# Two transformer blocks on one core: the experts' scatter and the next gather are emitted behind the following pair's gates

## The chip, the core and the metric

The kernel runs on one core of a Trainium2 chip. The metric is the device time of one execution in microseconds; the median of the runs is compared. The engines are TensorE (PE; its weight loads are listed apart as PEld), VectorE (DVE), ScalarE (ACT), GpSimd (POOL) and SyncE (SP), which issues most of the DMA transfers between the device's memory (HBM) and the on-chip SBUF. Matrix products land in PSUM.

## The reference, cut to what matters

The program is one block with two linear mixers and a mixture of experts, then a second block of two layers with attention and feed-forward. The change touches the experts alone: 256 tokens of 1024 features, 32 experts, of which each token takes the four with the largest logits. In words of the reference, per expert `e` on its rows `xb`:

```python
gu  = xb @ w_gu[e] + b_gu[e]
glu = jnp.minimum(gu[:, :D_EXPERT], SWIGLU_LIMIT)
lin = jnp.clip(gu[:, D_EXPERT:], -SWIGLU_LIMIT, SWIGLU_LIMIT)
act = glu * jax.nn.sigmoid(SWIGLU_ALPHA * glu) * (lin + 1.0)
return (act @ w_down[e] + b_down[e]) * p[:, None].astype(h.dtype)
```

The rows are added up at their tokens, and the sum times a gate `g2` is added to the residual. All weights are float32: 8 MB of gate and up weights and 4 MB of down weights an expert.

## The kernel before, in words

`phase1` is the mixer of the first block, `moe` the experts, `phase2` the second block. The change lies in `moe` (lines 1131 to 1389).

The 32 experts go in 16 pairs, 0 to 15, and two pairs make a block of four experts. Each expert has 64 slots for its tokens (`CAP`); the two experts of a pair lie side by side in the 128 rows of a matmul's output. What happens to a block and its pairs:

- **Gather** (lines 1323 to 1339). Two selection matrices `S` (VectorE, line 1325) of 128 tokens by 256 slots; then eight products of the normalized tokens (in two parts, `hl` and `hh`) with `S` on TensorE (line 1336), each into one of the two PSUM tiles `tr`, from which `scaled` (ScalarE line 1242, VectorE line 1244, in turn) writes an eighth of `xg`. `xg` is a tile of its own for odd blocks and lies in `resB` for even ones.
- **Gate and up** (line 1353). Eight steps, each of two pieces of weights (one of either expert, [128, 2048]) against an eighth of `xg`, into the PSUM tiles `gt` and `lt`; then the bias as a product (line 1357). These are the pair's gates.
- **Activation** (`swiglu`, lines 1250 to 1256). VectorE clamps `gt` to `g` and `lt` to `act`, ScalarE does three functions on `sg`, VectorE two more products. Eight transposes on TensorE (line 1263) and two copies on ScalarE (line 1264) turn the result to `aT`.
- **Down** (line 1373). Four steps of two pieces each, into `yd`.
- **Scatter** (lines 1266 to 1283). Two transposes of the slots' weights `sp` (line 1271), a copy to `spT`; VectorE multiplies `yd` by `g2` into `ys` (line 1277); four products of `spT` with `ys` (line 1280), each into one of the two tiles `tr`, and after each an addition to the residual `resA` on VectorE (line 1281).

The program emits this pair after pair: gather (in every second pair), gates, activation, down, scatter. A scheduler places the instructions of an engine in an order of its own, by its forecast of when each is ready, and an engine runs its own in that order. Where a conditional stands the order can't be mixed across it: ahead of pair 8 a branch (`overflow`, line 1292) looks whether an expert has more than 64 tokens; for these inputs it is not entered. The output biases of the experts are added in pair 6 (`biases`), and small preparations for the second block stand behind pairs 9, 11 and 13.

The weights come in 384 pieces of 1024 KB, which SyncE issues in order (line 1102) into a ring of 14 buffers (11 of `mring`, three of an older pool); a load waits until the products that read its buffer's last piece are done. Three more pieces are loaded ahead into a pool of their own at the start.

Of the kernel before, what the change touches and what calls it, by code (L numbers as in the profile page):

```python
# [9 lines left out]
F32 = mybir.dt.float32  # L10
# [10 lines left out]
# ---------------------------------------------------------------- constants that depend on shapes alone  # L21
def shape_constants():
# [9 lines left out]
    C["cum"] = np.concatenate([blk * (i[None] >= p[:, None]), blk * (i[None] <= p[:, None])], 1)   # within a chunk  # L32
    C["blk64"] = blk
    C["tri"] = (p[:, None] < i[None, :]).astype(np.float32)      # earlier tokens
    C["iota"] = np.broadcast_to(i.astype(np.float32), (128, 128)).copy()
    # rotary: swap of the halves of 64 dims, cos and signed sin over the 272 positions
# [7 lines left out]
def position_constants():  # L44
    """cos / signed sin [128, 2, 272], retention decays [128, 4, 656], and the buckets of the distances."""
# [4 lines left out]
    cos, sin = np.cos(ang).T, np.sin(ang).T                       # [32, T]  # L50
# [4 lines left out]
    dec = np.where(i >= j, np.exp(lg[:, None, None] * np.maximum(i - j, 0)), 0.0)     # [4, j, i]  # L55
# [4 lines left out]
    # table over m: distance m - 127, m = 0 .. 399  # L60
# [22 lines left out]
class K:  # L83
    """Handles shared by the parts of the program."""
# [5 lines left out]
    def c(self, pool, *names):  # L90
        """Load constants that lie side by side."""
        o = CONST_OFF[names[0]][0]
        n = CONST_OFF[names[-1]][0] + CONST_OFF[names[-1]][1] - o
        t = pool.tile([128, n], F32, name=self.nm("cst"), tag=self.nm("cst"), bufs=1)
        self.nc.sync.dma_start(t, self.a["cst"][:, o:o + n])
        r = [t[:, CONST_OFF[x][0] - o:CONST_OFF[x][0] - o + CONST_OFF[x][1]] for x in names]
        return r if len(r) > 1 else r[0]
# [6 lines left out]
class Halves:  # L104
    """[128, 8, 256] float32r as two tiles of four."""
# [9 lines left out]
def row_bcast(ap, parts, n):  # L115
    """A DRAM vector read onto every one of `parts` partitions."""
    return bass.AP(tensor=ap.tensor, offset=ap.offset, ap=[[0, parts], [1, n]])


def rsqrt_small(k, pool, out, v, n, parts=128, tag="rs", full=None):  # L120
    """out = v ** -0.5 on a small tile, with one Newton step after exp(-0.5 ln v)."""
# [15 lines left out]
LOW = -44.0                                                    # below it a sigmoid is under 1e-19, and Ln's range ends  # L137


def sigmoid(k, out, x):  # L140
    """out = 1 / (1 + exp(-x)) for x >= LOW."""
# [6 lines left out]
def split_hl(k, hi, lo, x):  # L148
    """x (float32) = hi + lo exactly, hi and lo in float32r."""
# [4 lines left out]
def mm3(nc, out, terms, start, stop):  # L154
    """The sum of float32 products w x as float32r ones, first those of the w's high parts.

    terms: (w high, w low, x high, x low, whether w is the stationary operand)."""
# [9 lines left out]
def load_w(k, src):  # L167
    """Weights of up to 1024 elements a partition: rows in tiles of 128."""
# [6 lines left out]
def parts(k, w):  # L175
    """The two float32r parts of a weight tile of 1024 elements a partition."""
# [7 lines left out]
# the order of the delta rule's steps. E: a group's decays on their way, P: the product of the next convolution, K, Q, V:  # L184
# convolutions, M: system matrices, X: a part of their inverses, H: what a head's scan takes, S: a step of the scan of two
# heads; k, q, v: projections of the linear attention, m: half of the modulation
DELTA_ORDER = "EkPPKPKPKPKMmXXXXXXXXXPQPQPVVHHkqSSSSSSSSPPQPQPVVHHSSSSSSSSEkPPKPKPKPKMXXXXXXXXXPQPQPVmVHHSSSSSSSSkPPQPQPVqqVHHSSSSSSSSqvv"
# the order of the linear attention's steps: D a head's decays and states, O its output, v values of a further head,
# S, G, R, b gates, B the normalized output
# [3 lines left out]
def phase1(k, A, B):  # L193
    """The mixer of the first block: x + g1*y by token in 2048 of 2176 columns of A; B is free after it.

    With it the norm's factor of a token (k.rstd), scale and shift of a feature (k.scale, k.shift) of the experts' input
    and the router's logits. Returns the experts' weights, with the first on their way."""
# [27 lines left out]
    # ------------------------------------------------ loads  # L225
# [3 lines left out]
    def big(shape, dt=F32):  # L229
        """2048 elements a partition."""  # L230
# [37 lines left out]
    adt = one.tile([128, 2, 16], F32, name="adt")                # a_log and dt_bias on every partition  # L268
# [9 lines left out]
    # ------------------------------------------------ modulation  # L278
# [14 lines left out]
    # ------------------------------------------------ normalized tokens, feature-major: [ctx | lat]  # L293
# [43 lines left out]
    def proj_fm(src, xh, xl):  # L337
        """128 output columns feature-major, [128, tokens of xh]."""
# [5 lines left out]
    def proj_tm(src, tiles, xh, xl, evac):  # L344
        """256 output columns token-major for the token tiles; evac(token tile, psum)."""
# [14 lines left out]
    # ------------------------------------------------ beta, decay gates, low-rank gates  # L360
# [12 lines left out]
    ba = B[0:48, 0:512]                     # beta's argument, and from row 32 the decay's  # L373
# [7 lines left out]
    tok = one.tile([128, 4, 3, 16], F32, name="tok")             # G, beta, exp(last - G) by token  # L381
# [6 lines left out]
    nc.scalar.activation(e1, e1, AF.Ln)                          # -ln beta  # L388
    # g = -exp(a_log) * softplus(a + dt_bias), log1p with its rounding made good
# [4 lines left out]
    nc.scalar.activation(e2, e2, AF.Exp, scale=-1.0)             # e = exp(-|x|)  # L394
    nc.vector.tensor_scalar_add(u1, e2, 1.0)                     # u = 1 + e
    nc.scalar.activation(g1, u1, AF.Ln)
    nc.vector.scalar_tensor_tensor(e2, u1, -1.0, e2, op0=ALU.add, op1=ALU.subtract)      # (u - 1) - e
# [5 lines left out]
    nc.vector.tensor_scalar_max(g1, g1, -104.0)                  # exp is zero there, and sums stay exact enough  # L403
# [8 lines left out]
    gb = one.tile([128, 4, 24], F32, name="gb")                  # G and G + ln beta (backward), to be turned to rows  # L412
# [50 lines left out]
    # ------------------------------------------------ convolution and its gate  # L463
# [11 lines left out]
    def conv_cols(ct):  # L475
        """Columns ct of q, k, v (24 tiles); its product may have been taken up before."""
# [42 lines left out]
    oa = B[:, 0:2048].rearrange("p (h t w) -> p t h w", h=8, t=2)            # its place is taken over by the experts' input  # L519
# [1506 lines left out]
```

## Time and profile before

| | |
|---|---|
| median of 3 runs | 2528.71 us (2528.28 to 2530.66) |
| the profiled execution, first to last instruction | 2534.7 us |
| mean granted TensorE clock | 0.958 of full speed |
| TensorE busy | 2342.3 us, 92% |
| VectorE, ScalarE, GpSimd busy | 1242.1, 924.1 and 118.7 us |
| moved by DMA | 605.9 MB, 239 GB/s in the mean |

The page gives for the profiled execution the busy time of each engine and, for 40 equal slices of 63.4 us, tenths of busy time. The profile shows a float32 matmul as two rows of TensorE, so the 72 gate and up matmuls of a pair (with the bias) are 144 rows. Experts run from about 750 to 1745 us: slices 12 to 28. The profile has no time of its own besides the span; the runs' median lies 6.0 us below it.

### The profile page before, as it was taken

What the parts mean: (1) busy time and instruction counts of PE and PEld (TensorE: products, weight loads), DVE (VectorE), ACT (ScalarE), POOL (GpSimd) and SP (SyncE); (2) the same over time, 40 slices, a digit from 0 to 9 for tenths busy, and PEclk for the clock granted to TensorE, in tenths of its full rate; (3) what the DMA queues carried; (4) which work ended last, traced back from release to release, by engine and by line L of the source; (5) the groups of instructions that cost most, each with busy time, mean ns of one, the idle gap of its engine ahead of it and who ended that gap; (6) DMA issues with size and microseconds to landing.
All of it is one profiled execution on the core that took longest, in us unless ns stands there. A gap on an engine that the chain in (4) does not pass through costs nothing.

```text
span 2534.7 us, 36527 instructions
## 1 busy us (share of the span) xinstructions
PE 2342.3 (92%) x14474; PEld 1550.9 (61%) x14475; DVE 1242.1 (49%) x2717; ACT 924.1 (36%) x1956; POOL 118.7 (5%) x156
## 2 busy tenths in 40 slices
PE   6699879999989999999899999998999999999998
PEld 3476557789873333333333333335878999878998
DVE  4988896677561111121211111114766556766655
ACT  4556555567430101010101010103455545455544
POOL 0112122000010000000000000000010000010000
PEclk8889988999989999999999999999999999999999
DMA  7522330234979999999899999995434555524563
GB/s 281 136 78 57 119 112 29 59 92 117 285 288 386 396 416 410 416 406 397 346 416 412 416 398 416 392 416 168 124 85 140 182 167 155 158 87 134 185 183 100
DMA packets 290349, 605.90 MB, mean 239 GB/s; under 512 B 26038, under 2 KB 218681, under 8 KB 254332
## 3 DMA queue, kind: packets, MB, share of 16 engines
q1 hardware_dynamic: 283236, 595.24, 64.1%
q10 hardware_dynamic: 6280, 7.80, 1.2%
q8 instruction: 116, 1.90, 0.3%
q0 software_dynamic: 656, 0.46, 0.1%
q14 instruction: 61, 0.50, 0.1%
HBM read 602.30 MB, written 1.15 MB: 238 GB/s over the span
## 4 chain that ended last, share of the span: by engine, by line
PE 33%; issue 14%; DVE 2%; ACT 1%; POOL 0%; DMA 0%; POOLq 0%; ACTq 0%; DVEq 0%
PE qm L164 13%; PE yd L1373 5%; PE gt L1353 4%; PE lt L1353 4%; PE tr L1280 1%; PE tr L1336 1%; PE gt L1357 0%; PE tr L1263 0%; PE qm L1759 0%; PE qm L1758 0%; DVE g L1250 0%; DVE act L1256 0%; PE ql L1822 0%; POOL bs L1775 0%; ACT sg L1254 0%
## 5 line engine op out<-in xcount | busy, mean ns | idle before, releaser
L150 ACT CAST wh<-w 128x1024 fp32r<-128x1024 f32 (+2 forms) x318 | 318.6, 1002 | 298.0 <-PE qm L164 203.2
L151 DVE TENSOR_TENSOR wl<-w,wh 128x1024 fp32r<-128x1024 f32 (+2 forms) x318 | 369.9, 1164 | 38.5 <-ACT wh L150 36.8
L164 PE MATMUL qm<-uh,wh 128*128 128x272 f32 (+2 forms) x1008 | 260.2, 292 | 0.1
L1373 PE MATMUL yd<-w,aT 128*64 128x512 f32 x1024 | 259.0, 637 | 0.9 <-ACT aT L1264 0.6
L164 PE MATMUL qm<-ul,wh 128*128 128x272 f32 (+2 forms) x1008 | 258.1, 289 | 0.0
L1250 DVE TENSOR_SCALAR g<-gt 128x1024 f32<-128x1024 f32 x16 | 19.6, 1224 | 409.5 <-PE gt L1357 353.9
L1252 ACT ACTIVATE sg<-g 128x1024 f32<-128x1024 f32 x16 | 16.9, 1057 | 538.5 <-DVE g L1250 538.5
L164 PEld LDWEIGHTS qm<-uh,wh 128*128 128x128 f32 (+1 forms) x1008 | 188.6, 187 | 7.6 <-issue 5.1
L164 PEld LDWEIGHTS qm<-ul,wh 128*128 128x128 f32 (+1 forms) x1008 | 189.2, 188 | 2.5 <-issue 0.7
L1353 PE MATMUL gt<-w,resB 128*64 128x512 f32 x512 | 183.3, 596 | 0.0
L1353 PE MATMUL lt<-w,resB 128*64 128x512 f32 x512 | 181.3, 593 | 0.6 <-DVE act L1251 0.6
L1353 PE MATMUL gt<-w,xg 128*64 128x512 f32 x512 | 178.3, 595 | 0.0
L1373 PEld LDWEIGHTS yd<-w,aT 128*64 128x64 f32 x1024 | 78.8, 148 | 161.4 <-issue 152.6
L1353 PE MATMUL lt<-w,xg 128*64 128x512 f32 x512 | 177.5, 593 | 0.0
L164 PE MATMUL qm<-uh,wl 128*128 128x272 f32 (+2 forms) x1008 | 147.7, 287 | 0.0
L164 PE MATMUL mm<-hTh,wh 128*128 128x256 f32 (+1 forms) x384 | 131.6, 362 | 8.8 <-ACT wh L150 4.1
L164 PEld LDWEIGHTS qm<-uh,wl 128*128 128x128 f32 (+1 forms) x1008 | 132.4, 187 | 0.7 <-issue 0.4
L164 PE MATMUL qm<-fl,wh 128*128 128x272 f32 (+1 forms) x512 | 128.6, 287 | 0.0
L164 PE MATMUL qm<-fh,wh 128*128 128x272 f32 (+1 forms) x512 | 128.4, 288 | 0.0
L164 PE MATMUL mm<-hTl,wh 128*128 128x256 f32 (+1 forms) x384 | 127.0, 350 | 0.0
L1353 PEld LDWEIGHTS lt<-w,resB 128*64 128x64 f32 x512 | 53.6, 137 | 73.0 <-issue 71.2
L1353 PEld LDWEIGHTS lt<-w,xg 128*64 128x64 f32 x512 | 53.4, 137 | 71.8 <-issue 71.4
(581 smaller groups left out, 4368.9 us busy)
## 6 DMA issues: line engine op xcount, KB each, us to landing
w<-in_w_gu_dram SPq DMA_DIRECT2D x256, 1024.0 KB
w<-in_w_down_dram SPq DMA_DIRECT2D x128, 1024.0 KB
w<-in_w_ff_dram SPq DMA_DIRECT2D x64, 1024.0 KB
w<-in_w_in_dram SPq DMA_DIRECT2D x72, 512.0 KB
w<-in_w_in_dram SPq DMA_DIRECT2D x30, 1024.0 KB
y<-in_w_mod_dram SPq DMA_DIRECT2D x19, 1024.0 KB
w<-in_w_out_dram SPq DMA_DIRECT2D x24, 512.0 KB
w<-in_w_mod_dram SPq DMA_DIRECT2D x5, 1024.0 KB
```

The costliest lines, as they stand in the source:

```text
L150: k.nc.scalar.copy(hi, x)
L151: k.nc.vector.tensor_sub(lo, x, hi.bitcast(F32))
L164: nc.tensor.matmul(out, l, r, start=start and n == 1, stop=stop and n == 3 * len(terms))
L1250: nc.vector.tensor_scalar(g, gt, 7.0, LOW / 1.702, op0=ALU.min, op1=ALU.max)
L1252: nc.scalar.activation(sg, g, AF.Exp, scale=-1.702)
L1280: nc.tensor.matmul(o, spT[:, t * 128:(t + 1) * 128], ys[:, js], start=True, stop=True)
L1336: nc.tensor.matmul(o, hx[:, t, f * 128:(f + 1) * 128], S[t].rearrange("p e s -> p (e s)"), start=(t == 0 and i == 0), stop=(t == 1 and i = ...
L1353: nc.tensor.matmul(quarter(j)[64 * i:64 * i + 64], xg[:, kk, c0:c0 + CAP], w[i][:, j * 512:(j + 1) * 512], start=(kk == 0), stop=False)
L1373: nc.tensor.matmul(yd[64 * i:64 * i + 64, j * 512:(j + 1) * 512], aT[:, 2 * f2 + f, 64 * i:64 * i + 64], w[i][:, f, j * 512:(j + 1) * 512] ...
```

## The change

It splits the loop into functions (`gather`, `gate_up`, `down`, `taken`) and emits them in another order. `taken` is the product of `yd` with `g2`, which was a part of `scatter`; it now follows the down products at once. The scatter of a pair is emitted only after the next pair's gates and activation, and so is the gather of the next block, in the second pair of a block. Pair 7's scatter stays ahead of the branch, block 4's gather behind it, and pair 15's scatter is the last. The rest of the textual difference takes out comments.

```diff
-    def scatter(sp, yd, fn=None):
+    def taken(yd):
+        ys = wk.tile([128, 1024], F32, name=k.nm("ys"), tag="ys", bufs=2)
+        for j in range(2):
+            js = slice(j * 512, j * 512 + 512)
+            nc.vector.tensor_mul(ys[:, js], yd[:, js], g2r[:, js])
+        return ys
+
+    def scatter(sp, ys, fn=None):
...
-        ys = wk.tile([128, 1024], F32, name=k.nm("ys"), tag="ys", bufs=2)
         for j in range(2):
             js = slice(j * 512, j * 512 + 512)
-            nc.vector.tensor_mul(ys[:, js], yd[:, js], g2r[:, js])
...
-    for b in range(8):
-        if b == 4:
-            posm = overflow()
+    def gather(b):
...
-            if e0 == 12:
-                biases(weights_T())
-            act = wk.tile([128, 1024], F32, name=k.nm("act"), tag="act", bufs=1)
-            swiglu(gt, lt, act)
-            aT = act_T(act)
...
-            scatter(sp, yd, squares if e0 == 30 else None)
...
+    last = None
+    for n in range(16):
+        b, e0 = n // 2, 2 * n
+        if n == 8:
+            scatter(*last)
+            last = None
+            posm = overflow()
+        if n in (0, 8):
+            S, xg = gather(b)
...
+        gt, lt = gate_up(e0, xg)
...
+        swiglu(gt, lt, act)
+        if last is not None:
+            scatter(*last)
+        if n % 2 and n not in (7, 15):
+            S, xg = gather(b + 1)
+        if n == 6:
+            biases(weights_T())
+        last = sp, taken(down(act_T(act)))
+        if e0 in (18, 22, 26):
+            q = next(setup)
+    scatter(*last, squares)
```

What the scheduler makes of it on TensorE, at three places. The names are those of the sections above; the numbers are the tiles' own. First, before the change, from pair 3's last down products to block 2's gather:

```order
L1373 MATMUL yd_8670<-w_8707,aT_8657 64x512
L1373 MATMUL yd_8670<-w_8709,aT_8657 64x512
L1280 MATMUL tr_8726<-ys_8724,spT_8722 128x512
L1280 MATMUL tr_8729<-ys_8724,spT_8722 128x512
L1280 MATMUL tr_8733<-ys_8724,spT_8722 128x512
L1280 MATMUL tr_8736<-ys_8724,spT_8722 128x512
L1336 MATMUL tr_8743<-S_8739,hl 128x256
L1336 MATMUL tr_8743<-S_8739,hh 128x256
L1336 MATMUL tr_8743<-S_8741,hl 128x256
L1336 MATMUL tr_8743<-S_8741,hh 128x256
L1336 MATMUL tr_8749<-S_8739,hl 128x256
```

The four scatter products follow the down products, and the gather follows them; pair 4's first gate matmul comes after three of the gather's eight tiles.

After the change, from pair 2's last down product on, in pair 3's gates (line 1357 is gate and up, line 1286 the scatter):

```order
L1373 MATMUL yd_8469<-w_8508,aT_8456 64x512
L1357 MATMUL gt_8524<-w_8526,xg_8206 64x512
L1357 MATMUL lt_8525<-w_8526,xg_8206 64x512
L1286 MATMUL tr_8645<-ys_8518,spT_8643 128x512
L1286 MATMUL tr_8648<-ys_8518,spT_8643 128x512
L1357 MATMUL gt_8524<-w_8528,xg_8206 64x512
L1357 MATMUL gt_8524<-w_8526,xg_8206 64x512
L1357 MATMUL gt_8524<-w_8528,xg_8206 64x512
L1357 MATMUL lt_8525<-w_8528,xg_8206 64x512
L1357 MATMUL lt_8525<-w_8526,xg_8206 64x512
L1357 MATMUL lt_8525<-w_8528,xg_8206 64x512
L1286 MATMUL tr_8651<-ys_8518,spT_8643 128x512
```

Two gate matmuls now stand between the down products and pair 2's scatter, and six between its two halves. Block 2's gather (line 1342) follows in and behind pair 3's second and third gate steps, in groups of 7, 9, 11 and 5 products with gate matmuls in between.

The third place, after the change, is the end of pair 3's gates (line 1362 is the bias):

```order
L1357 MATMUL lt_8525<-w_8612,xg_8206 64x512
L1362 MATMUL gt_8524<-bgu,cst_61 64x512 x4
L1362 MATMUL lt_8525<-bgu,cst_61 64x512 x4
L1263 MATMUL tr_8710<-cst_61,act_8630 128x128 x4
L1263 MATMUL tr_8716<-cst_61,act_8630 128x128 x4
L1373 MATMUL yd_8722<-w_8723,aT_8709 64x512
```

Between the bias products and the transposes of the activation nothing stands, as before the change. In pair 1 alone most of block 1's gather stands there. The order of SyncE's loads is the same in both kernels.

## Rows read from the trace of the kernel before

**Rows 1.** The page: span, busy time of the engines, transfers' tenths in 40 slices.
```profile
span 2534.7 us, 36527 instructions
...
PE 2342.3 (92%) x14474; PEld 1550.9 (61%) x14475; DVE 1242.1 (49%) x2717; ACT 924.1 (36%) x1956; POOL 118.7 (5%) x156
...
DMA  7522330234979999999899999995434555524563
```

**Rows 2.** Stretches: us, busy time (rows) of PE to POOL, PEclk, DMA share, GB/s.
```profile
785.60:1715.00 929.40, 847.79 (x3632) 304.29 (x3630) 167.18 (x232) 86.22 (x118) 1.09 (x2) 0.96 0.99 402
785.60:840.50 54.90, 52.28 (x229) 18.85 (x226) 9.44 (x13) 4.62 (x6) 0.00 (x0) 1.00 0.94 382
840.50:905.50 65.00, 59.82 (x258) 22.39 (x258) 12.31 (x19) 6.97 (x10) 0.00 (x0) 0.95 0.99 397
905.50:964.10 58.60, 53.55 (x228) 18.30 (x226) 9.34 (x13) 4.71 (x6) 0.00 (x0) 0.94 1.02 416
1214.00:1286.10 72.10, 61.11 (x260) 23.74 (x258) 14.25 (x25) 6.97 (x10) 0.00 (x0) 0.93 0.88 355
```

**Rows 3.** DMA issues of the experts' weights: count, size of each.
```profile
w<-in_w_gu_dram SPq DMA_DIRECT2D x256, 1024.0 KB
w<-in_w_down_dram SPq DMA_DIRECT2D x128, 1024.0 KB
```

**Rows 4.** Waits of SyncE, 785.6 to 1715 us: us in total, times, longest.
```profile
SPq L1102 <- PE lt L1353: 398.2, 207, 21.3
SPq L1102 <- PE yd L1373: 288.8, 67, 16.5
...
SPq L1292 <- SPq L1292: 16.1, 6, 5.3
```

**Rows 5.** The weight tiles `w`: idle time of their readers until (us, times).
```profile
  DMA w<-in_w_gu_dram: 7.4, 23
```

**Rows 6.** Stretches at the experts' end, and VectorE's first row behind the last product.
```profile
1715.00:1720.00 5.00, 1.72 (x8) 0.27 (x2) 4.05 (x4) 3.17 (x3) 0.00 (x0) 1.00 0.65 257
1720.00:1725.00 5.00, 3.96 (x16) 1.78 (x18) 0.85 (x1) 1.13 (x2) 0.00 (x0) 0.68 0.00 0
...
1739.03 1.29 DVE L1277 TENSOR_TENSOR ys<-yd,g2r 128x512 f32<-128x512 f32 x2 [18.18 <-PE yd L1373]
```

**Rows 7.** Timeline of TensorE, pair 2: start, us, instructions [idle before, released by].
```profile
894.88 1.45 PE L1353 MATMUL lt<-w,xg 128*64 128x512 f32 x5
...
898.32 1.45 PE L1353 MATMUL lt<-w,xg 128*64 128x512 f32 x5
...
911.25 1.97 PE L1263 MATMUL tr<-cst,act 128*128 128x128 f32 x8 [4.18 <-DVE act L1256]
913.14 12.88 PE L1373 MATMUL yd<-w,aT 128*64 128x512 f32 x50
...
930.85 3.86 PE L1280 MATMUL tr<-ys,spT 128*128 128x512 f32 x8 [0.87 <-DVE ys L1277]
934.64 1.50 PE L1353 MATMUL gt<-w,xg 128*64 128x512 f32 x5
```

**Rows 8.** Timeline of TensorE: block 1's gather, its first rows and what follows it.
```profile
869.69 0.38 PE L1336 MATMUL tr<-S,hl 128*128 128x256 f32 x1
869.91 0.28 PE L1336 MATMUL tr<-S,hh 128*128 128x256 f32 x1
870.03 0.28 PE L1336 MATMUL tr<-S,hl 128*128 128x256 f32 x1
...
877.67 1.50 PE L1353 MATMUL lt<-w,xg 128*64 128x512 f32 x5
```

**Rows 9.** Timeline of TensorE: the first row behind the branch ahead of pair 8.
```profile
1248.40 0.55 PE L1336 MATMUL tr<-S,hl 128*128 128x256 f32 x1 [5.92 <-DVE sp L1343]
```

**Rows 10.** Stretches behind an activation and around a scatter (columns as in rows 2).
```profile
911.20:916.20 5.00, 4.95 (x16) 2.58 (x18) 0.00 (x0) 1.17 (x2) 0.00 (x0) 0.50 1.01 419
930.00:934.60 4.60, 3.75 (x8) 1.27 (x8) 3.35 (x5) 0.00 (x0) 0.00 (x0) 1.00 1.02 420
```

More of the change, by code (lines that the diff above doesn't have):

```diff
@@ L1338, in moe @@
             scaled(xg[:, f, :], o, f)
-        for pr in range(2):
-            e0 = 4 * b + 2 * pr
-            sp = wk.tile([128, 2, 128], F32, name=k.nm("sp"), tag="sp", bufs=2)
-            for t in range(2):
-                nc.vector.tensor_tensor(sp[:, t, :].rearrange("p (e s) -> p e s", e=2), S[t][:, 2 * pr:2 * pr + 2, :].bitcast(F32),
-                                        prob[:, t, e0:e0 + 2].unsqueeze(2).to_broadcast([128, 2, CAP]), op=ALU.mult)
-            gt = ps.tile([128, 1024], F32, name=k.nm("gt"), tag="gt", bufs=1)
-            lt = ps.tile([128, 1024], F32, name=k.nm("lt"), tag="lt", bufs=1)
-            quarter = lambda j: (gt, gt, lt, lt)[j][:, (j % 2) * 512:(j % 2) * 512 + 512]
-            for kk in range(8):
-                w = weights.two()
-                for j in range(4):
-                    for i in range(2):
-                        c0 = (2 * pr + i) * CAP
-                        nc.tensor.matmul(quarter(j)[64 * i:64 * i + 64], xg[:, kk, c0:c0 + CAP],
-                                         w[i][:, j * 512:(j + 1) * 512], start=(kk == 0), stop=False)
+        return S, xg
@@ L1355, in moe, with gate_up @@
+    def gate_up(e0, xg):
+        gt = ps.tile([128, 1024], F32, name=k.nm("gt"), tag="gt", bufs=1)
+        lt = ps.tile([128, 1024], F32, name=k.nm("lt"), tag="lt", bufs=1)
+        quarter = lambda j: (gt, gt, lt, lt)[j][:, (j % 2) * 512:(j % 2) * 512 + 512]
+        for kk in range(8):
+            w = weights.two()
             for j in range(4):
                 for i in range(2):
-                    nc.tensor.matmul(quarter(j)[64 * i:64 * i + 64], ident[:, 32 * j + e0 + i:32 * j + e0 + i + 1].to_broadcast([128, 64]),
-                                     bgu, start=False, stop=True)
@@ L1359, in moe @@
-            if e0 == 0:
-                early.__exit__(None, None, None)
-                wk.late = P("mlate", reuse_waits="tile")
-            if e0 == 12:
-                biases(weights_T())
-            act = wk.tile([128, 1024], F32, name=k.nm("act"), tag="act", bufs=1)
-            swiglu(gt, lt, act)
-            aT = act_T(act)
-            yd = ps.tile([128, 1024], F32, name=k.nm("yd"), tag="yd", bufs=1)
-            for f2 in range(4):
-                w = weights.two()
-                for f in range(2):
-                    for j in range(2):
-                        for i in range(2):
-                            nc.tensor.matmul(yd[64 * i:64 * i + 64, j * 512:(j + 1) * 512],
-                                             aT[:, 2 * f2 + f, 64 * i:64 * i + 64], w[i][:, f, j * 512:(j + 1) * 512],
-                                             start=(f2 == 0 and f == 0), stop=(f2 == 3 and f == 1))
@@ L1376, in moe @@
-            scatter(sp, yd, squares if e0 == 30 else None)
-            if e0 in (18, 22, 26):
-                q = next(setup)
+                    c0 = (e0 % 4 + i) * CAP
+                    nc.tensor.matmul(quarter(j)[64 * i:64 * i + 64], xg[:, kk, c0:c0 + CAP],
+                                     w[i][:, j * 512:(j + 1) * 512], start=(kk == 0), stop=False)
+        for j in range(4):
+            for i in range(2):
+                c = 32 * j + e0 + i
+                nc.tensor.matmul(quarter(j)[64 * i:64 * i + 64], ident[:, c:c + 1].to_broadcast([128, 64]),
+                                 bgu, start=False, stop=True)
@@ new lines, in gate_up, with down @@
+        return gt, lt
+    def down(aT):
+        yd = ps.tile([128, 1024], F32, name=k.nm("yd"), tag="yd", bufs=1)
+        for f2 in range(4):
+            w = weights.two()
+            for f in range(2):
+                for j in range(2):
+                    for i in range(2):
+                        nc.tensor.matmul(yd[64 * i:64 * i + 64, j * 512:(j + 1) * 512],
+                                         aT[:, 2 * f2 + f, 64 * i:64 * i + 64], w[i][:, f, j * 512:(j + 1) * 512],
+                                         start=(f2 == 0 and f == 0), stop=(f2 == 3 and f == 1))
+        return yd
@@ new lines, in moe @@
+    last = None
[7 more added lines that the diff above has]
+            S, xg = gather(b)
+        sp = wk.tile([128, 2, 128], F32, name=k.nm("sp"), tag="sp", bufs=2)
+        for t in range(2):
+            nc.vector.tensor_tensor(sp[:, t, :].rearrange("p (e s) -> p e s", e=2), S[t][:, e0 % 4:e0 % 4 + 2, :].bitcast(F32),
+                                    prob[:, t, e0:e0 + 2].unsqueeze(2).to_broadcast([128, 2, CAP]), op=ALU.mult)
+        gt, lt = gate_up(e0, xg)
+        if n == 0:
+            early.__exit__(None, None, None)
+            wk.late = P("mlate", reuse_waits="tile")
+        act = wk.tile([128, 1024], F32, name=k.nm("act"), tag="act", bufs=1)
+        swiglu(gt, lt, act)
[8 more added lines that the diff above has]
+            q = next(setup)
@@ L1444, in big_expert @@
                              start=(f == 0), stop=(f == 7))
-    L["scatter"](sp, yd)
+    L["scatter"](sp, L["taken"](yd))
 def phase2_setup(k, one, tmp, psum):
```

## The prediction

> **What bounds the kernel now.** I read the page first. Over 2534.7 us TensorE is busy 92% of the time, and the digits of the transfers stand at 9 in the middle of the span, where the experts run: both look full there [rows 1]. So the next view is the table of stretches, cut from one pair's gates to the next's (each stretch begins where the 16-times repeated clamp of line 1250 starts). From pair 0's gates to pair 15's are 929.4 us, 62.0 us a pair. A pair takes 24 pieces of 1024 KB [rows 3], 25.17 MB, which at 416 GB/s need 60.5 us. An undisturbed pair (905.5 to 964.1) runs at 416 GB/s and no stretch goes visibly above it, but the mean over the 15 pairs is 402 [rows 2]. The weight queue therefore works 97% of the stage: TensorE, at 62.0 us a pair, is slower than the supply by a narrow 1.5 us.
>
> Who waits for whom agrees. SyncE, which issues the loads, waited 398.2 and 288.8 us in this stage for the products on lines 1353 and 1373 to give a buffer back [rows 4]; TensorE waited 7.4 us in all, 23 times, for gate and up weights [rows 5]. The last byte of the experts lands near 1718 us (1715 plus 0.65/1.02 of five; nothing afterwards), and the last down product ends just ahead of 1739.0: the weights lay ready, a stock of 20.8 us [rows 6]. **TensorE's own sequence is the bound now, with the transfers 2.4% behind it.**
>
> **What the change does to TensorE's sequence.** A gate step of two pieces is 16 matmul rows and takes 3.44 us (894.88 to 898.32), 0.215 us each. After a pair's down products TensorE stands 0.87 us for VectorE's product with g2, then spends 3.79 us (930.85 to 934.64) on eight scatter rows whose work is 8 x 0.215 = 1.72 us, since each waits for an addition to empty one of two PSUM tiles [rows 7]. In the new order two gate matmuls (four rows, 0.86 us) stand ahead of the first scatter, and six (2.6 us) between its halves; the wait for g2's product, 0.87 us, and that for two additions are covered. Saved: 0.87 + 3.79 - 1.72 = 2.9 us a scatter. 14 of 16 are moved (those of pairs 7 and 15 stay): 41 us.
>
> The gather takes 869.69 to 877.67, 7.98 us, in which stand ten rows of gates (2.15 us) and 32 of its own at 0.115 us (869.91 to 870.03), 3.7 us [rows 8]. The other 2.1 us are stalls. It is still alternated with gate matmuls on two PSUM tiles, only in longer groups, so between 0 and 2.1 us go; nothing in the trace has just this pattern, and I take half, 1.1 us, for each of six gathers: 6 us. Together the change frees about **47 us of TensorE** (41 to 53).
>
> What it doesn't free: the 4.18 us in which TensorE stands for the activation, ahead of the transposes on line 1263 [rows 7], 60 us over the stage. The words of the source put scatter and gather just there, but the printed order has nothing between the bias products and these transposes, save in pair 1. The multiplication, now `taken`, only moves into its own function; VectorE and ScalarE do the same work, off the path. No DMA is added or moved, SyncE's order of loads is the same. The branch ahead of pair 8 stays as it is, with its own scatter in front and gather behind: TensorE's 5.92 us there [rows 9] are still paid.
>
> **What the transfers let through.** A pair without gather falls from 58.6 us [rows 2] to 55.7 and one with it comes to 55.7 + 3.7 + 1.1 = 60.5, 58.1 on average, below the 60.5 us of its weights. So the stock is used up within some pairs and then the supply decides. Counted from the supply: before, it lost 929.4 x (1 - 402/416) = 31.3 us between the two gates [rows 2]. Of these, 4.5 are in the first stretch (54.9 x (1 - 382/416)), where loads wait for pair 0's products, which don't move, and about 1 us of the second one is that too: not to be had. The largest part, 72.1 x (1 - 355/416) = 10.6 us, is pair 8's stretch, where SyncE stands 16.1 us in the branch [rows 4] and later finds full buffers. With the stock used up, most of the 14 buffers (35 us of transfers) are in the queue when SyncE enters the branch, so I count this as regained; if not, it stays lost. The supply then regains 31.3 - 5.5 = 25.8 us.
>
> The stock itself is the other term. At the end a supply-bound TensorE uses the last gate pieces as they land. Then come that step (3.4), bias products (3.4), the activation (4.2), transposes (1.9, 911.25 to 913.14), four down steps (13.8, transposes 0.4, and 2.1 at the lowered clock: 50 rows took 12.88 us for 10.75) [rows 7]: 29.2 us, while the last eight pieces need 20.1. So 9.1 us are left behind the last byte at the least and 20.8 at the most; I take the lower end, since TensorE is then the one that waits: 20.8 - 9.1 = 11.7 us. The sum: 25.8 + 11.7 = **37.5 us**, less than the 47 that TensorE frees. What follows the experts waits for the last down product in both kernels and shifts whole.
>
> The profiled span of 2534.7 us would become 2497.2; the runs' median of 2528.71 lies 6 us below that span, so I take the 37.5 from it: **2491.2 us**.
>
> On the supply's rate: the full stretch runs at 416 GB/s [rows 2]. The Trainium skill, DMA: Bandwidth & Descriptors, section Measured, has 425 GB/s for large loads on a core alone; by that figure a pair's supply would be 59.2 us, my estimate some 15 us lower in all, and the 47 us of TensorE would nearly all be seen. This trace doesn't show such a rate.
>
> **The rivals.**
> *TensorE stays the bound, or the branch loses as before (part of the gain).* If only the 0.87 us wait is saved in each scatter, it is 14 x 0.87 = 12 us: 2516.5. If the branch's 10.6 us and half of the stock's term stay, it is 37.5 - 10.6 - 5.9 = 21 us: 2507.7. For it: the new groups of the gather have not been timed. Against: two PSUM tiles are enough for the pattern of two scatters, six gates, two scatters.
> *The transfers hide it (no change).* If 402 GB/s were all that the queue gives, nothing would come of it: 2528.7. For: digits of 9, a load share of 0.99. Against: 416 in full stretches, and SyncE's 687 us of waiting for TensorE.
> *Slower, by the clock.* TensorE would now wait between gate steps. After the 4.18 us of standing, the clock was 0.50 from 911.2 to 916.2 us; at that level a step takes 6.9 us, more than the 5.04 in which its pieces come. If short waits had the same effect, each step at the low clock adds 3.4 us to the 58.1: from (62.0 - 58.1)/3.4 = 1.1 such steps a pair it is slower than now, and at two a pair (64.9 us against 62.0, 15 times) it is 2572. Against it: around the scatter, from 930.0 to 934.6, with eight rows of 1.72 us in 4.6 us, the clock was 1.00 [rows 10], and a supply-bound gate step works 3.44 of 5.04 us, a larger part; a low clock would also end the waits that caused it. The Trainium skill, TensorE: Matmul & The Clock Gate, section HAM oscillation, describes a matmul kernel in which the waits for transfers put the clock back on every K tile; by that rule this rival would be the outcome, and the row around the scatter speaks against it here.
> *The change doesn't do what it says.* The scheduler could have put everything back; the printed order excludes that, and shows only that the activation's gap stays empty. With the supply as the bound, a filled gap would give the same time.
>
> **How the numbers follow.** Forecast (27 to 46 us saved): 0.67. Part of the gain (6 to 27): 0.17. More than 46, by a faster supply: 0.04. No change: 0.06. Slower: 0.06. A measurement of this kernel can tell about 0.2%, 5 us, from no change. The range runs from 2482.5 (46 saved: the first stretch's 4.5 us too, and a rate higher by 0.4%) to 2514 (15 saved, between the two forms of the partial gain); it leaves out the 0.04 below, some 0.04 of the partial gain, and the 0.12 of the last two cases. Faster 0.87, same 0.07, slower 0.06.
>
> **What would show it.** Right: the stretch from pair 0's to pair 15's gates near 904 us in place of 929.4, 416 GB/s in most pairs' stretches and also in pair 8's; TensorE's wait for gate weights up from 7.4 to about 25 us or more; the 0.87 us ahead of each scatter gone; the activation's 4.18 us still there; the last product some 9 us behind the last byte. Wrong: TensorE's waits for weights as small as before with stretches of 58 us or more (gather or scatter stall in their new places), a clock at 0.50 between gate steps, or stretches at 402 GB/s with an idle SyncE.

## The result, and the profile after

The changed kernel takes 2559.84 us (median of 4 runs, 2555.3 to 2561.4) against 2529.26 before (4 runs): a ratio of 1.0116, 95% interval 1.0102 to 1.0129. It is **slower by 1.2%**; forecast were 2491.2 us and a range of 2482.5 to 2514. The page of the changed kernel (span, busy time of the engines, transfers in tenths of 40 slices):

```profile
span 2553.5 us, 36514 instructions
...
PE 2370.4 (93%) x14474; PEld 1582.0 (62%) x14475; DVE 1243.5 (49%) x2717; ACT 923.0 (36%) x1956; POOL 117.9 (5%) x156
...
DMA  7532321225989999999899999995424555524663
```

TensorE has as many rows as before, 14474, and VectorE and ScalarE did the same work in the same time, but TensorE is busy 28.1 us longer (2342.3 in [rows 1]). The same products cost more. The table of stretches, cut at the clamp of line 1250 as in [rows 2]: the whole stage, pair 3's and pair 4's gates, and the stretch of the branch.

```profile
778.50:1729.40 950.90, 881.55 (x3630) 339.37 (x3628) 166.13 (x232) 85.77 (x118) 1.09 (x2) 0.96 0.97 393
...
897.40:964.90 67.50, 62.95 (x260) 25.17 (x258) 11.68 (x17) 6.97 (x10) 0.00 (x0) 0.97 0.99 404
964.90:1023.00 58.10, 53.91 (x228) 20.42 (x226) 9.37 (x13) 4.71 (x6) 0.00 (x0) 0.97 0.98 398
1213.40:1286.10 72.70, 61.59 (x262) 23.66 (x260) 14.36 (x25) 6.87 (x10) 0.00 (x0) 0.91 0.87 352
```

The stage grew from 929.4 to 950.9 us. Two opposite things are in it. TensorE's idle time fell from 929.40 - 847.79 = 81.6 us to 950.90 - 881.55 = 69.4, by 12.3; its busy time rose by 33.8 with practically the same number of rows. The granted clock is 0.96 in both, the branch's stretch is as long as before, and a pair without a gather takes 58.1 us where [rows 2] has 58.6: nothing came of the 2.9 us. A pair that holds a gather takes 67.5. Transfers fell to 393 GB/s, but TensorE did not wait for them: 6.5 us in all for gate and up weights, 14 times, against 7.4 in [rows 5]. They were slowed by buffers that came free later: SyncE waited 436.1 and 319.3 us in the stage for the products of gates and down, where [rows 4] has 398.2 and 288.8.

The two profiles differ by 18.8 us: 21.5 in the stage, 7.1 less ahead of it, 4.4 more behind it. The runs' medians differ by 30.6; the stretch ahead of the stage varies between executions (it ends at 774 to 788 us in the runs below), and what the 4.4 are is open.

Where the busy time went is seen on the timeline of TensorE at the second place of the printed orders above, pair 3's first gate steps (a float32 matmul is two rows):

```profile
920.03 0.59 PE L1357 MATMUL gt<-w,xg 128*64 128x512 f32 x1
920.46 0.59 PE L1373 MATMUL yd<-w,aT 128*64 128x512 f32 x1
920.46 0.59 PE L1357 MATMUL gt<-w,xg 128*64 128x512 f32 x1
920.89 1.02 PE L1357 MATMUL lt<-w,xg 128*64 128x512 f32 x2
921.92 1.95 PE L1286 MATMUL tr<-ys,spT 128*128 128x512 f32 x4
923.81 1.50 PE L1357 MATMUL gt<-w,xg 128*64 128x512 f32 x5
924.72 0.64 PE L1357 MATMUL lt<-w,xg 128*64 128x512 f32 x1
925.15 0.59 PE L1357 MATMUL gt<-w,xg 128*64 128x512 f32 x1
925.20 2.25 PE L1357 MATMUL lt<-w,xg 128*64 128x512 f32 x5
927.38 1.98 PE L1286 MATMUL tr<-ys,spT 128*128 128x512 f32 x4
929.30 1.07 PE L1357 MATMUL gt<-w,xg 128*64 128x512 f32 x2
930.21 1.02 PE L1357 MATMUL lt<-w,xg 128*64 128x512 f32 x2
931.16 0.39 PE L1342 MATMUL tr<-S,hl 128*128 128x256 f32 x1
...
936.81 0.38 PE L1342 MATMUL tr<-S,hl 128*128 128x256 f32 x1 [0.19 <-ACT resB L1242]
...
937.47 1.07 PE L1357 MATMUL gt<-w,xg 128*64 128x512 f32 x2
```

A whole gate step is 16 rows in 3.44 us [rows 7]. Here four rows take 1.89 us (920.03 to 921.92), twelve take 3.57 (923.81 to 927.38), four 1.86 (929.30 to 931.16). The column with the array's shape tells why. A gate or down matmul is `128*64`: it fills 64 of the array's 128 columns, those of its expert (one expert's output lies in rows 0 to 63 of PSUM, the other's in 64 to 127). Two rows of different halves run at the same time (at 920.46 a `yd` and a `gt` row start together), so eight pairs of rows of 0.43 us make the 3.44. Scatter and gather are `128*128`, full-width in what follows: nothing runs beside them. In the changed order, two matmuls of one expert stand ahead of the scatter. The first, `gt`, runs here beside the last two rows of the down products; the second, `lt`, has no partner. Of the six behind, four are the other expert's: 8 x 0.43 = 3.44 us for that half, while the first half has four rows. This became **theory A: the halves lose their partners where a full-width product stands between them.** Against it stood theory B (waits for PSUM tiles that VectorE and ScalarE empty) and theory C (transfers slower by themselves).

### The profile page after: what moved, and what is told of

It reads as the page before. It is cut to its first block, busy times and chain, and to the rows that moved or that the text cites. A ratio compares the mean times of both kernels' runs of the same rounds, so it can differ in the third digit from the quotient of the medians.

```text
span 2553.5 us, 36514 instructions
## 1 busy us (share of the span) xinstructions
PE 2370.4 (93%) x14474; PEld 1582.0 (62%) x14475; DVE 1243.5 (49%) x2717; ACT 923.0 (36%) x1956; POOL 117.9 (5%) x156
## 4 chain that ended last, share of the span: by engine, by line
PE 33%; issue 14%; DVE 2%; ACT 1%; POOL 0%; DMA 0%; POOLq 0%; ACTq 0%; DVEq 0%
PE qm L164 13%; PE yd L1373 5%; PE gt L1357 4%; PE lt L1357 4%; PE tr L1286 1%; PE tr L1342 1%; PE tr L1263 1%; PE gt L1362 0%; PE qm L1788 0%; PE qm L1787 0%; DVE act L1256 0%; DVE g L1250 0%; PE ql L1851 0%; POOL bs L1804 0%; PE ql L1613 0%
## 5 line engine op out<-in xcount | busy, mean ns | idle before, releaser
L1357 PE MATMUL lt<-w,resB 128*64 128x512 f32 x512 | 194.0, 594 | 0.6 <-DVE act L1251 0.6
L1357 PE MATMUL lt<-w,xg 128*64 128x512 f32 x512 | 191.3, 593 | 0.0
L1357 PEld LDWEIGHTS lt<-w,resB 128*64 128x64 f32 x512 | 59.0, 137 | 77.2 <-issue 75.8
L1357 PEld LDWEIGHTS lt<-w,xg 128*64 128x64 f32 x512 | 60.9, 137 | 73.2 <-issue 73.2
```

The costliest lines, as they stand in the source:

```text
L1357: nc.tensor.matmul(quarter(j)[64 * i:64 * i + 64], xg[:, kk, c0:c0 + CAP], w[i][:, j * 512:(j + 1) * 512], start=(kk == 0), stop=False)
```

## The experiments

Before, in all groups of runs: 2526.9 to 2537.6 us. Stage is from the first to the last clamp of line 1250 (exact starts, so up to 0.1 us off the windows above), busy is TensorE's on the page. Whole steps means that the eight matmuls of a gate step are chained, so that nothing can stand within one.

| kernel | median us | ratio to before (95%) | stage us | busy us |
|---|---|---|---|---|
| before | 2529.3 | | 929.5 | 2342.3 |
| changed | 2559.8 | 1.0116 (1.0102 to 1.0129) | 951.0 | 2370.4 |
| e1 changed, whole steps | 2506.4 | 0.9900 (0.9880 to 0.9921) | 906.3 | 2314.3 |
| e2 scatter alone moved | 2555.0 | 1.0094 (1.0073 to 1.0116) | 954.9 | 2368.4 |
| e3 gather alone moved | 2545.4 | 1.0050 (1.0034 to 1.0067) | 940.4 | 2355.4 |
| e4 before, whole steps | 2512.0 | 0.9926 (0.9901 to 0.9950) | 912.8 | 2314.3 |
| d1 added product, halves even | 2530.8 | 0.9994 (0.9984 to 1.0004) | 928.8 | 2339.4 |
| d2 added product, halves odd | 2568.0 | 1.0140 (1.0117 to 1.0163) | 961.2 | 2369.2 |
| e5 scatter in the gap, whole steps | 2502.7 | 0.9880 (0.9860 to 0.9901) | 901.1 | 2313.4 |
| e6 as e5, gather between steps | 2504.0 | 0.9881 (0.9856 to 0.9906) | 901.0 | 2307.6 |
| e7 the change's places, halves even | 2511.2 | 0.9923 (0.9906 to 0.9940) | 911.0 | 2330.8 |
| e5b scatter in the gap alone | 2506.6 | 0.9909 (0.9889 to 0.9930) | 900.4 | 2336.7 |

**Whole steps, and each half of the change alone.** The edit of e1 in `gate_up` (`chain` adds a dependency in order of issue alone; e4 has the same edit in the kernel before):

```diff
-            w = weights.two()
+            w, m = weights.two(), None
             for j in range(4):
-                for i in range(2):
+                for i in (1, 0):
...
-                    nc.tensor.matmul(quarter(j)[64 * i:64 * i + 64], xg[:, kk, c0:c0 + CAP],
-                                     w[i][:, j * 512:(j + 1) * 512], start=(kk == 0), stop=False)
+                    m = chain(k, nc.tensor.matmul(quarter(j)[64 * i:64 * i + 64], xg[:, kk, c0:c0 + CAP],
+                                                  w[i][:, j * 512:(j + 1) * 512], start=(kk == 0), stop=False), m)
```

> The changed kernel, but the eight matmuls of a gate step are chained in the order of issue (both experts alternating, the first one needs the second piece), so that scatter and gather can stand between gate steps only, not within one. Theory A (split steps): a gate or down matmul fills half of the array's 128 columns and runs beside one of the other expert; a full-width product within a step leaves the halves unpaired, about 2 us for each split step (four rows 1.9 us for 0.86, twelve rows 3.6 for 2.6). Counting halves over the printed order (0.86 us a half matmul, 0.90 a scatter matmul, 0.116 a gather row) the 15 pairs take 940 us in the changed kernel, 899 before and 873 here, without waits; the wait for g2's product (0.87 us) and for the copy of the transposed selection come back in most pairs, some 15 us. So about 50 us less than the changed kernel's 2559.8, bounded below by the weights' supply: 2505 to 2520. A step next to a scatter takes 3.5 us in the trace. Theory B (PSUM): the time goes to products that wait for VectorE or ScalarE to empty one of two PSUM tiles; the gather's groups are longer here (15 and 17 products in a row): no gain, 2555 to 2570. Theory C (supply): the transfers became slower by themselves; their order is the same here: 2555 to 2562.

Measured: 2506.4 us, 53 less than the changed kernel and 1.0% less than before. Theories B and C are out: the groups of scatter and gather are longer than in the change, the order of the loads is the same, and the loss is gone. The timeline of e1 at pair 3's first steps (line 1294 is the scatter, 1365 gate and up, 1350 the gather):

```profile
913.25 3.86 PE L1294 MATMUL tr<-ys,spT 128*128 128x512 f32 x8 [0.55 <-ACT spT L1289]
917.04 1.94 PE L1365 MATMUL gt<-w,xg 128*64 128x512 f32 x8
918.81 1.89 PE L1365 MATMUL lt<-w,xg 128*64 128x512 f32 x8
920.62 0.39 PE L1350 MATMUL tr<-S,hl 128*128 128x256 f32 x1
```

Sixteen gate rows take 3.58 us (917.04 to 920.62), right between a scatter and a gather. The eight scatter rows take 3.79 (913.25 to 917.04) as in [rows 7]; that is eight times 0.43 and little more, so it is work and not waiting.

e2 and e3 put one half of the change back:

```diff
-        if n in (0, 8):
+        if n % 2 == 0:
             S, xg = gather(b)
...
-        if n % 2 and n not in (7, 15):
-            S, xg = gather(b + 1)
```

> The changed kernel with the gather put back to its old place (at the head of a block): the scatter alone is moved. Theory A: the printed order has two split gate steps round most scatters and three round the gather; counting halves gives 939 us for the 15 pairs, against 940 in the changed kernel and 899 before, and the 0.87 us wait of the kernel before is covered: 2553 to 2562, so nearly the whole loss is there with the scatter alone. Theory B: the gather is as before, and only a share of the loss is left, by 14 scatters to 6 gathers at most two thirds of it: 2540 to 2550. Theory C says nothing on this.

```diff
-        if last is not None:
-            scatter(*last)
...
-        last = sp, taken(down(act_T(act)))
+        scatter(sp, taken(down(act_T(act))), squares if n == 15 else None)
```

> The kernel with the scatter put back behind its own pair's down products; the gather alone is moved. Theory A: four split places round each moved gather instead of three, one split round the scatter as before: counting halves gives 913 us for the 15 pairs against 899 before and 940 in the changed kernel; the 0.87 us wait stays: 2538 to 2545, slower than before (2529) and faster than the changed kernel. Theory B (two gathers' stalls): 2535 or less.

> The kernel before, with the eight matmuls of each gate step chained as in the first experiment; nothing else. Theory A: the kernel before has split steps as well (one gate matmul ahead of the odd pairs' scatters, odd groups between the gather's tiles); counting halves gives 877 us in place of 899 for the 15 pairs, less some 8 us for the transposed selection's copy, which is no longer covered: 12 to 16 us less than 2529, so 2512 to 2518. Theories B and C: nothing changes, 2527 to 2532.

Measured: 2555.0, 2545.4 and 2512.0. All three lie in the ranges of theory A or within 0.4 us of them, and outside those of theory B. The scatter alone brings nearly the whole loss, the gather alone 0.5%; the two do not add up, since each order splits other steps (counted below). The kernel before had split steps too: whole ones give it 0.74%. The change's own idea, with whole steps in both kernels, is then worth 2512.0 - 2506.4 = 6 us, and the intervals of the two overlap.

**The price by itself.** In steps 3 and 5 (counted from 0) of each pair of e4, one useless full-width product behind the second matmul; the sources of d1 and d2 differ in the order of the halves alone.

```diff
+                for n, (j, i) in enumerate(((0, 1), (0, 0), (1, 1), (1, 0), (2, 1), (2, 0), (3, 1), (3, 0))):
...
+                    if n == 1 and kk in (3, 5):
+                        m = chain(k, nc.tensor.transpose(tr(128), ident, ident), m)
```

In d2 the table is `((0, 0), (2, 0), (0, 1), (1, 0), (1, 1), (2, 1), (3, 0), (3, 1))`.

> A price by itself. The kernel before with whole gate steps (experiment e4), and in steps 3 and 5 of each pair one full-width product of no use (128 columns, a transposed identity, one row) behind the step's second matmul. The halves of the array alternate in issue, 1 0 | 1 0 1 0 1 0 (the bar is the added product), so no matmul loses its partner. This adds work to the computation. Theory A (halves without partner): the step takes 3.44 us plus the product's 0.2 to 0.4: 3.6 to 3.9 us between the steps' first matmuls; the time is 2512 plus up to 12, 2513 to 2524. A theory that any full-width product within a step costs 2 us by itself (a change of the array's form, a reloading of weights): 5.4 us for such a step, 2550 or more.

> As the run before, the same added product at the same place, but the matmuls of a step in the scheduler's own order of halves, 0 0 | 1 0 1 1 0 1, so that at the bar two of one half have run alone. Theory A: 1.72 us for the first two and 3.44 for the six, 5.2 plus 0.2 to 0.4 in place of 3.44: 5.4 to 5.6 us for a step with the product and 3.4 for one without; 32 such steps and odd groups round the gather: 70 to 90 us more than the run before's 2513 to 2524, 2585 to 2605. The other theory: no difference between these two runs.

Measured: 2530.8 and 2568.0. TensorE's line on the page, d1 and then d2:

```profile
PE 2339.4 (92%) x14506; PEld 1548.8 (61%) x14507; DVE 1241.4 (49%) x2717; ACT 923.4 (36%) x1956; POOL 118.2 (5%) x156
```

```profile
PE 2369.2 (92%) x14506; PEld 1579.8 (62%) x14507; DVE 1243.9 (48%) x2717; ACT 924.5 (36%) x1956; POOL 117.8 (5%) x156
```

The same products, the added ones at the same places, 29.8 us of TensorE and 37 us of time apart: the order of the halves makes the difference. Not all of it arises at the added products. In d2 the scheduler also puts the transposes of `sp` within the down products, and the gather's tiles into other groups; by the count below, some 14 us belong to the added products and the rest to such places. But my sizes missed on both sides. d1's step is as forecast, 3.85 us from its first row to the next step's (941.09 to 944.94):

```profile
941.09 1.03 PE L1360 MATMUL gt<-w,xg 128*64 128x512 f32 x4
942.05 0.33 PE L1363 MATMUL tr<-cst 128*128 128x128 f32 x1
942.31 1.08 PE L1360 MATMUL gt<-w,xg 128*64 128x512 f32 x4
943.22 1.89 PE L1360 MATMUL lt<-w,xg 128*64 128x512 f32 x8
944.94 1.89 PE L1360 MATMUL gt<-w,xg 128*64 128x512 f32 x8
```

Thirty-two such steps give 13 us; measured were 19 over e4, 16 of them in the stage, and the rest is open. In d2 I had charged each split step for itself. Its two splits partly make up for each other: between the two added products either half has the same number of matmuls, and only what stands ahead of the first and behind the second is uneven. So theory A took a better form: **between two full-width products, the half with more rows counts.** Counted like this over the printed orders, d2 takes 34 us more than d1 (measured 37) and the changed kernel 28 more than before (busy time: 28.1 on the page, 33.8 in the stage). The same count gives e2 23 us and e3 9 us over before; their stages are 25.5 and 11.0 us longer.

**The same places, even halves.** e7 forces scatter and gather to the places that the change gave them and alternates the halves:

```diff
+GROUPS = {(1, 0): 7, (1, 3): 9, (2, 0): 11, (2, 3): 5}
...
+                for i in (1, 0):
...
+                if products is not None and kk == 0 and j in (0, 3):
+                    m = products((j // 3,), m)
+                if rows is not None and (kk, j) in GROUPS:
+                    for _ in range(GROUPS[kk, j]):
+                        m = chain(k, next(rows), m)
```

> The changed kernel's order with one thing changed: scatter and gather stand at the very places of the change (behind two gate matmuls and behind eight, the gather in groups of 7, 9, 11 and 5), in all of the 14 and 6 pairs, but the matmuls of a step alternate between the halves, 1 0 | 1 0 1 0 1 0 in place of 0 0 | 1 0 1 1 0 1. Theory A, now in the form that the pair of runs with the added product left (what is paid is, between two full-width products, the half with more matmuls): a step with products behind two matmuls is 0.86 + 2.58 in place of 1.72 + 3.44; counting the longer half over the printed orders gives 886 us for the 15 pairs, 927 in the changed kernel. The transposes of the selection no longer lie within the down products, up to 0.5 us a pair back. 28 to 41 us less than the changed kernel's 2559.8: 2518 to 2532. Theories by place (products within a step cost 2 us, PSUM tiles, transfers): 2553 or more.

Measured: 2511.2 us, 49 less than the changed kernel, more than forecast; in the profiles the stage is 40.0 us shorter and TensorE 39.6 us less busy, at the upper end. Its timeline in pair 3, to be read beside that of the changed kernel (1381 gate and up, 1297 scatter, 1360 gather):

```profile
920.33 1.08 PE L1381 MATMUL gt<-w,xg 128*64 128x512 f32 x4
921.34 1.98 PE L1297 MATMUL tr<-ys,spT 128*128 128x512 f32 x4
923.25 1.08 PE L1381 MATMUL gt<-w,xg 128*64 128x512 f32 x4
924.16 1.89 PE L1381 MATMUL lt<-w,xg 128*64 128x512 f32 x8
925.98 1.98 PE L1297 MATMUL tr<-ys,spT 128*128 128x512 f32 x4
927.89 1.08 PE L1381 MATMUL gt<-w,xg 128*64 128x512 f32 x4
928.90 0.39 PE L1360 MATMUL tr<-S,hl 128*128 128x256 f32 x1
...
933.69 0.39 PE L1360 MATMUL tr<-S,hl 128*128 128x256 f32 x1 [0.19 <-ACT resB L1251]
...
934.36 1.08 PE L1381 MATMUL gt<-w,xg 128*64 128x512 f32 x4
```

Four gate rows take 1.01 us in place of 1.89 (there two of them ran beside down rows), twelve 2.73 in place of 3.57, four 1.01 in place of 1.86; the scatter's groups take 1.91, as there. So full-width products may stand within a step; what costs is that halves are left without partner. This settles the cause.

**The gap.** TensorE still stood 4.2 us for the activation in nearly every pair. e5 has whole steps and queues the scatter behind the pair's last bias product; e5b has this edit alone; e6 adds to e5 the gather's tiles between gate steps, two behind each of steps 1 to 4, counted from 0.

```diff
-        gt, lt = gate_up(e0, xg)
+        gt, lt, bias = gate_up(e0, xg)
...
         if last is not None:
-            scatter(*last)
+            with tc.issue_after(bias):
+                scatter(*last)
```

> The changed kernel with whole gate steps, and the scatter's transposes and products queued on TensorE behind the last bias product of the pair that follows, where TensorE stands 4.18 us for the activation (the scheduler then puts the gather there too). Theory A: no step is split, the wait for g2's product is gone and the scatter's 3.8 us lie in the gap. Counting halves gives 812 us of TensorE for the 15 pairs, below the 15 x 60.5 = 907 us of the weights: the supply is the bound, and the part of the prediction that went from there to 2491 can be seen: 2485 to 2498. If the additions of scatter and gather delay the activation on VectorE and ScalarE, the gap grows, still under the supply's pace. Rival (clock): TensorE waits for weights between steps, its clock falls to 0.50 there, and the time stays above 2505. Theories B and C: 2530 or more.

> As the run before, but with the gather's eight tiles between gate steps of the odd pair, two tiles behind each of steps 1 to 4, and the scatter alone in the gap. Theory A: TensorE has 819 us of work for the 15 pairs, still below the supply: the same as the run before within 5 us, 2483 to 2498, since the supply is the bound. If the gap behind the bias is what limits (additions of scatter and gather ahead of the activation), it is faster than the run before by more.

> The changed kernel with one edit: the scatter is queued on TensorE behind the last bias product of the pair that follows, where TensorE stands for the activation; the gate steps are left to the scheduler. The printed order then has 64 gate matmuls in a row in nearly every pair, with the scatter and the gather behind the bias. Theory A: as in experiment e5 (2502.7), within 6 us: 2497 to 2509, since nothing stands within a step any more and the weights' supply is the bound. If chaining the steps had a merit of its own, 2515 or more.

Measured: 2502.7, 2504.0 and 2506.6, all under both kernels and equal within their spread; e5 and e6 are 5 and 6 us above the top of what I expected. The stage in the profiles is 900 to 901 us in all three. The timeline of e5 at the end of pair 2's gates (1370 bias, 1287 and 1294 scatter, 1271 the activation's transposes, 1381 down):

```profile
897.72 1.89 PE L1370 MATMUL lt<-bgu,cst 128*64 128x512 f32 x8
899.53 0.44 PE L1287 MATMUL tr<-cst,sp 128*128 128x128 f32 x2
900.56 1.98 PE L1294 MATMUL tr<-ys,spT 128*128 128x512 f32 x4 [0.59 <-ACT spT L1289]
902.86 1.12 PE L1294 MATMUL tr<-ys,spT 128*128 128x512 f32 x2 [0.32 <-DVE resA L1295]
904.59 1.13 PE L1294 MATMUL tr<-ys,spT 128*128 128x512 f32 x2 [0.61 <-DVE resA L1295]
905.56 0.60 PE L1271 MATMUL tr<-cst,act 128*128 128x128 f32 x4
906.50 0.66 PE L1271 MATMUL tr<-cst,act 128*128 128x128 f32 x4 [0.34 <-DVE resA L1295]
907.09 13.95 PE L1381 MATMUL yd<-w,aT 128*64 128x512 f32 x64
920.87 1.89 PE L1365 MATMUL gt<-w,xg 128*64 128x512 f32 x8
```

From the bias to the down products are 7.56 us (899.53 to 907.09) with a whole scatter in them; in [rows 7] it was 4.18 and 1.89 without. So a scatter costs 1.5 us here, where behind the down products it cost 0.87 + 3.79. TensorE's waits in e5 and then five stretches of it: the stage, the first 5 us of the down products above, and the experts' end.

```profile
PE gt L1365 <- DMA w<-in_w_gu_dram: 42.9, 32, 2.7
```

```profile
788.20:1689.40 901.20, 812.99 (x3622) 287.70 (x3620) 156.89 (x229) 82.68 (x117) 1.09 (x2) 0.98 1.01 411
907.10:912.10 5.00, 5.00 (x25) 1.76 (x26) 0.00 (x0) 0.59 (x1) 0.00 (x0) 1.00 1.04 423
1695.00:1700.00 5.00, 4.05 (x19) 1.84 (x20) 2.17 (x4) 1.17 (x2) 0.00 (x0) 1.00 0.97 386
1700.00:1705.00 5.00, 5.00 (x26) 1.66 (x24) 0.00 (x0) 0.00 (x0) 0.00 (x0) 1.00 0.29 116
1705.00:1710.00 5.00, 5.00 (x26) 1.65 (x24) 0.00 (x0) 0.00 (x0) 0.00 (x0) 1.00 0.00 0
```

TensorE now waits for weights, and the supply is the bound. TensorE's busy time no longer matters: e5b, whose steps are not chained, is 23 us busier than e5 and has the same stage. By the count its odd halves are worth only 4 us; most of the rest is that it begins a step with the piece that lands first, one half alone, where e5 stands until both are there: its waits for gate weights are 13.4 us, not 42.9. Nor do the runs tell e5 from e1 (2502.6 to 2507.9 us against 2501.4 to 2512.1), in which the gap stays empty: filling it is not shown to gain time once the steps are whole.

## Why the prediction was wrong

**What bounds the kernel: right.** TensorE's sequence was the bound and the supply close behind it, as e5 shows.

**"2.9 us a scatter", 41 us in all: the step that failed.** It had three parts.
- The 0.87 us wait for g2's product did go. Of TensorE's waits in the stage, before and then after, this is most of the 12.3 us by which its idle time fell:

```profile
PE tr L1280 <- DVE ys L1277: 12.2, 14, 0.9
```

```profile
PE tr L1286 <- DVE ys L1272: 1.8, 2, 0.9
```

- "Eight scatter rows whose work is 8 x 0.215 = 1.72 us, since each waits for an addition" was false. 0.215 us is a gate row's share of a pair that runs side by side. A full-width row has no partner and takes 0.43; the eight take 3.79 us in e1 and twice 1.9 in e7 and in the change. The 2.07 us of stalls, 14 times 29 us, did not exist.
- "Two gate matmuls (four rows, 0.86 us) and six (2.6 us)" took 1.89 and 3.57 us (the 1.89 with two down rows beside them). I had taken a mean from undisturbed steps for matmuls that I had myself printed in an order that splits them. e7 puts the whole of it at 40 us of TensorE, the gather's part and some odd groups among the down products included.

**"1.1 us a gather": wrong in sign.** Of the 7.98 us, 2.1 were called stalls. The timeline before names no wait there: the ten gate rows take 3.02 us in three groups in place of 2.15 (one group is a single matmul without partner, 1.00 us for two rows), and the gather's 32 rows 4.96 in place of 3.7, with 0.22 us from the first row of a group to the second where later ones follow at 0.12. The rest of the 4.96 is open. In the change the second gate step, with sixteen of the gather's products in it, takes 8.17 us (929.30 to 937.47), in e7 6.47 (927.89 to 934.36), and both have the same short wait for a PSUM tile, 0.19 us.

**The supply's part: three quarters of it came, once TensorE was really freed.** Forecast were 25.8 us of supply and 11.7 of stock. In e5 the last byte lands near 1701.4 us (1700 plus 0.29/1.02 of five), 913.2 after the first clamp, where it was 932.6 before: 19.4 us. The last down product ends just ahead of 1712.3, so 11 us behind the last byte in place of 20.8: 10 us. Together 29 of 37.5; the medians of e5 and before differ by 29.8, though the profiled execution is the longest of e5's four, 2512.1 us. The branch's stretch is what I had counted on too much: 69.8 us in e5 between the clamps of pairs 7 and 8, 72.1 before, so 2.3 of the 10.6 us were regained.

**The rivals.** The outcome was slower, but by none of mine. The clock rival asked for a TensorE that waits for weights more than before; the changed kernel waits no longer (6.5 us), and e5, which does (32 waits, the longest 2.7 us), has a clock of 0.98 over the stage. The Trainium skill, TensorE: Matmul & The Clock Gate, section HAM oscillation, describes waits for transfers that put the clock back on every K tile. The waits of that page's example are longer than any of these 32, so e5 neither bears it out nor speaks against it; to forecast this rival from it went beyond the page. The sign that I had named for a failure, waits for weights as small as before with stretches of 58 us or more, is what came, though "gather or scatter stall" was not the reason.

**What could have been read before.** [rows 7] has sixteen rows of `128*64` in 3.44 us and eight of `128*128` in 3.79, with the shapes beside them, and the printed order shows which piece each gate matmul reads. The Trainium skill, TensorEngine Tiling (Array Packing), section Key Properties, says that changing the tiling mode drains TensorE. The trace fits that, without showing a drain as such: in e7 four paired rows take 1.01 us where a whole step has 0.86 for four, so some 0.15 us go at such a change. The change of mode is the small part; the lost partners are the large part, since a matmul without one takes 0.86 us for itself.

## What to carry to other kernels

Where matmuls fill half of the array, as here, the time of a stretch between two full-width products is that of the half with more rows; count the halves in the order that is really issued before costing a product that is moved between them. Keep partners next to each other, and put full-width work where the engine stands anyway (here that freed TensorE, and no time shows it, since the supply bounds by then). A mean from an undisturbed stretch is no price for the same instructions in another neighbourhood, and a difference between two kinds of rows is no stall until their shapes have been compared.

## What was not expected of the hardware

The two halves keep their own pace. In the changed kernel the matmuls behind the scatter are issued as `gt`, `gt`, `gt`, `lt`, `lt`, `lt`, the fourth and the sixth of the same expert as the third. The first row of `lt` starts at 924.72, beside the third matmul's first row, and must be the fifth's, since the fourth needs the half that the third still holds; the record of the next `lt` row (925.20) has the semaphore update that the fifth carries and the fourth does not. A later matmul passed an earlier one.

Filling the gap also raised the clock behind it. After 4.18 us of standing, the clock was 0.50 ([rows 10]) and the down products with two transposes took 913.14 to 929.98, 16.84 us [rows 7]; in e5, where the scatter fills the gap, the clock is 1.00 over their first 5 us and they take 13.8 us (907.09 to 920.87), with no transposes among them. In e5 this is not seen in the time, since TensorE then waits for weights.
